# Target as fp32 on SyncE's queue, pred as bf16 on GpSimd's queue, both on the same DMA engines

## The chip, the core and the metric

The kernel runs on one core of a Trainium2 chip. The metric is the device time of one execution in microseconds (us). Engines are named as the profile names them: PE (TensorE, matmuls), PEld (its weight loads), DVE (VectorE), ACT (ScalarE), POOL (GpSimd), SP (SyncE). A DMA is issued from a queue, here SP's or POOL's, and moved by the core's 16 DMA engines.

## What is computed

Masked-patch reconstruction loss for 32 samples of 147 rows with 768 elements each, with the target normalised per row:

```python
mean = target.mean(axis=-1, keepdims=True)
var = target.var(axis=-1, keepdims=True)
target = (target - mean) / np.sqrt(var + 1e-6)
loss = np.mean((pred - target) ** 2, axis=-1)   # (32, 147)
return loss.mean(axis=-1)                       # (32,)
```

pred and target are fp32, 14.45 MB each. A sum of squares over everything is wanted, one number per sample.

## The kernel before

**Layout.** The 147 rows of a sample are spread over four partitions, 37 rows each for the first three and 36 for the fourth, so that 32 samples fill 128 partitions. "Column" c (0 to 35) is the c-th row of every partition: 128 x 768 elements. Column 36, called `REST` (`KM` = 36 is the same number), exists on 96 partitions only. All of target and pred has room in SBUF, so no load waits for a buffer.

**Work on one column.** DVE takes `bn_stats` over two halves of 384 and `bn_aggr` (mean, variance), for a *group* of columns; ACT takes the Sqrt of the group's variances; DVE makes 1/sqrt (`r`) and -mean/sqrt (`nmr`); that is `stats(g)`. POOL normalises a column to bf16, s = t * r + nmr (`normalise`). For a *unit* of two columns (the last two and `REST` are units of one) PE forms z = p - s in PSUM by matmuls against a negative and a positive identity (`subtract`: three matmuls on s, three on p for a pair), and ACT squares z and sums it along the row (`square`). Small matmuls against a mask add the partitions of a sample (`sums`), DVE adds up, and SP stores 32 numbers. PSUM holds two z at a time; the `work` pool holds ten normalised units.

**Loads.** Each piece of one to four columns is one DMA; each of its partition rows is contiguous in DRAM (12 KB for four fp32 columns). Only two pieces, target's `REST` and columns 0 to 3, go over SP's queue, as fp32. All others are issued by POOL, which casts fp32 to bf16 on the way: four bytes are read for two written. The list `stream` alternates target and pred pieces, target some eight columns ahead, and ends with smaller pieces. POOL's loads share eight completion semaphores in turn, so a ninth load waits for the first to land; `lanes` in the planner models that.

**Order.** Every instruction is pinned to the order of the program. A planner in Python computes a due time for each step from modelled landings (`land`) and modelled durations, collects the steps with `at(when, fn)`, and emits them sorted by due time. So what runs on each engine, and what stands behind what in its queue, follows from the modelled landings, not from the actual ones. POOL's queue holds loads and normalisations together; ACT's holds the Sqrts and the squares together.

Of the kernel before, what the change touches and what calls it, by code (L numbers as in the profile page):

```python
# [7 lines left out]
F32 = mybir.dt.float32  # L8
BF16 = mybir.dt.bfloat16
# [5 lines left out]
def kernel(  # L15
# [7 lines left out]
    nc = tc.nc  # L23
    pin = tc.keep_in_program_order
    B, N, D = pred.shape
    eps = 1e-6
    P = 128
    J = P // B
    KJ = (N + J - 1) // J
    KM = N - (J - 1) * KJ  # L30
# [4 lines left out]
    REST = KM  # L35
# [4 lines left out]
    def rows_of(c):  # L40
        return RP if c == REST else P

    def dram(x, c0, c1):
        return bass.AP(tensor=x.tensor, offset=x.offset + c0 * D,
                       ap=[[N * D, B], [KJ * D, J - 1 if c0 == REST else J], [1, (c1 - c0) * D]])

    data = ctx.enter_context(tc.tile_pool(name="data", bufs=1))
# [4 lines left out]
    psum1 = ctx.enter_context(tc.tile_pool(name="psum1", bufs=1, space=bass.MemoryType.PSUM))  # L52


    stream = [("t", REST, REST + 1, "hw"), ("t", 0, 4, "hw"), ("p", REST, REST + 1, "sw")]
    stream += [("t", 4, 8, "sw"), ("t", 8, 12, "sw"), ("p", 0, 4, "sw")]
    for c in range(12, KM - 4, 4):
        stream += [("t", c, c + 4, "sw"), ("p", c - 8, c - 4, "sw")]
    stream += [("t", KM - 4, KM - 2, "sw"), ("p", KM - 12, KM - 8, "sw"), ("t", KM - 2, KM, "sw"),
               ("p", KM - 8, KM - 6, "sw"), ("p", KM - 6, KM - 4, "sw"), ("p", KM - 4, KM - 2, "sw"),  # L60
               ("p", KM - 2, KM - 1, "sw"), ("p", KM - 1, KM, "sw")]

    units = [(REST,)] + [(c, c + 1) for c in range(0, KM - 2, 2)] + [(KM - 2,), (KM - 1,)]

    groups = [(REST,)] + [tuple(range(c, c + 4)) for c in range(0, KM - 8, 4)]
    groups += [(c, c + 1) for c in range(KM - 8, KM, 2)]


    land, issue = {}, []
    t = 2.7  # L70
    for kind, c0, c1, q in stream:
        t += (c1 - c0) * D * 4 * rows_of(c0) / 430e3
        issue.append(t + 1.0)
        for c in range(c0, c1):
            land[kind, c] = t + 1.0

    todo = []

    def at(when, fn):
        todo.append((when, len(todo), fn))  # L80

    tbuf, pbuf, sbuf, rs = {}, {}, {}, {}

    def load(kind, c0, c1, q):
        x = targ_f if kind == "t" else pred_f
        n = rows_of(c0)
        til = data.tile([P, (c1 - c0) * D], F32 if q == "hw" else BF16, name=f"{kind}{c0}")
        eng = nc.sync if q == "hw" else nc.gpsimd
        pin(eng.dma_start(out=til[:n], in_=dram(x, c0, c1)))  # L89
        for c in range(c0, c1):  # L90
            (tbuf if kind == "t" else pbuf)[c] = (til, (c - c0) * D)

    lanes = [0.0] * 8
    k = 0
    for i, piece in enumerate(stream):
        if piece[3] == "hw":
            at(-1.0, lambda piece=piece: load(*piece))
        else:
            at(lanes[k % 8] + (0.01 * k), lambda piece=piece: load(*piece))
            lanes[k % 8] = issue[i] + 0.2  # L100
            k += 1

    ident = singles.tile([P, P], BF16)
    nident = singles.tile([P, P], BF16)
# [100 lines left out]
    for u in units:  # L205
# [7 lines left out]
        i = main_units.index(u) if u in main_units else -1  # L213
# [47 lines left out]
```

## Time and profile before

| | us |
|---|---|
| median of 3 runs (81.06 to 81.78) | 81.3 |
| the profiled execution | 80.73 |
| its span, first to last instruction | 79.0 |
| busy: POOL / DVE / PE / ACT | 50.1 / 45.7 / 38.7 / 32.5 |
| share of POOL's queue in the time of 16 DMA engines | 84.2% |
| share of SP's queue | 6.2% |

How to read it: busy times are sums over the span, and no engine is above 63% of it. The profile names lines of the kernel (L140 `bn_stats`, L142 Sqrt, L144 `nmr`, L158 `normalise`, L178 `subtract`, L184 `square`, L89 the loads), the tiles by the program's names (`t`, `p`, `s`, `z`), and in brackets the idle time before an instruction with what ended it. GB/s counts the bytes that a DMA writes. In the changed kernel all lines are 12 higher, the loads excepted, which go from L89 to L106.

### The profile page before, as it was taken

Reading aid. Unit: us, or ns where it says so; the run is one execution under the profiler, and the core shown is the slowest. Engines: PE = TensorE matmul, PEld = TensorE weight load, DVE = VectorE, ACT = ScalarE, POOL = GpSimd, SP = SyncE. Lnnn points to the kernel's source line nnn. Section 1 sums busy time; section 2 is a strip of 40 time slices with the busy share of each in tenths; the row PEclk is TensorE's granted clock in tenths of the full one; section 3 lists DMA queues with packets and bytes.
Section 4 is the critical chain, followed back from the end, with each engine's and each line's share of the span. In section 5 each row is a group of like instructions: output and inputs, shape, how many; then the busy total and the mean of one; then the engine's idle time right before and its main releaser. Section 6 shows DMA issues by size and latency. Waiting matters only on the chain.

```text
span 79.0 us, 602 instructions
## 1 busy us (share of the span) xinstructions
PE 38.7 (49%) x126; PEld 13.4 (17%) x126; DVE 45.7 (58%) x137; ACT 32.5 (41%) x53; POOL 50.1 (63%) x73
## 2 busy tenths in 40 slices
PE   0000330008990069985317980991399496496500
PEld 0000210001320023231102320320131031223300
DVE  0061039979799799797797089529779267000000
ACT  5000000050100590872931760583134873999700
POOL 4998802059789899897797795399779360800000
PEclk9999999999999655599965569759956999999996
DMA  0799999999999999999999999999999999990000
GB/s 0 182 412 317 311 218 218 211 218 218 211 215 218 211 216 218 211 211 218 218 211 215 218 215 209 221 215 211 205 227 202 210 210 220 199 165 4 0 0 0
DMA packets 3444, 15.43 MB, mean 195 GB/s; under 512 B 432, under 2 KB 784, under 8 KB 3312
## 3 DMA queue, kind: packets, MB, share of 16 engines
q0 software_dynamic: 3136, 13.52, 84.2%
q1 hardware_dynamic: 304, 1.87, 6.2%
q14 instruction: 3, 0.02, 0.1%
q8 instruction: 1, 0.02, 0.1%
HBM read 28.90 MB, written 0.00 MB: 366 GB/s over the span
## 4 chain that ended last, share of the span: by engine, by line
DMA 42%; DVE 31%; ACT 7%; POOL 5%; PE 4%; issue 4%; SPq 1%; ACTq 0%
DMA p<-in_pred_dram 30%; DVE st L140 23%; DMA t<-in_target_dram 12%; DVE mv L141 5%; ACT z L184 5%; POOL s L158 5%; PE z L178 4%; ACT r L142 2%; DVE r L143 1%; DVE nmr L144 1%; SPq L89 1%; POOL t L89 1%; PE acc L190 0%; DVE ob L224 0%; ACTq L256 0%
## 5 line engine op out<-in xcount | busy, mean ns | idle before, releaser
L140 DVE BATCH_NORM_STATS2 st<-t 128x6 f32<-128x384 bf16 (+2 forms) x74 | 36.3, 533 | 14.4 <-DMA t<-in_target_dram 14.4
L158 POOL TENSOR_SCALAR s<-t,r,nmr 128x768 bf16<-128x768 bf16 (+2 forms) x37 | 35.9, 976 | 13.3 <-DVE nmr L144 13.0
L178 PE MATMUL z<-s,nident 128*128 128x512 bf16 (+3 forms) x57 | 21.4, 492 | 26.6 <-POOL s L158 23.7
L184 ACT ACTIVATE z<-z 128x1536 f32<-128x1536 f32 (+2 forms) x20 | 26.7, 1336 | 2.0 <-PE z L178 2.0
L178 PE MATMUL z<-p,ident 128*128 128x512 bf16 (+3 forms) x57 | 20.6, 478 | 8.9 <-DMA p<-in_pred_dram 8.9
L142 ACT ACTIVATE r<-mv,eps_t 128x4 f32<-128x4 f32 (+2 forms) x12 | 3.6, 296 | 39.4 <-DVE mv L141 39.4
L178 PEld LDWEIGHTS <-nident 128*128 128x128 bf16 (+1 forms) x57 | 5.8, 117 | 39.5 <-ACT z L184 16.3
L89 POOL DMA_DIRECT2D p<-in_pred_dram x13 | 7.7, 594 | 5.2 <-DMA t<-in_target_dram 3.2
L178 PEld LDWEIGHTS <-ident 128*128 128x128 bf16 (+1 forms) x57 | 7.0, 123 | 20.5 <-issue 17.8
L141 DVE BATCH_NORM_AGGREGATE mv<-st 128x2 f32<-128x12 f32 (+1 forms) x37 | 7.7, 208 | 1.3
L89 POOL DMA_DIRECT2D t<-in_target_dram x9 | 5.3, 589 | 0.0
L143 DVE RECIPROCAL r<-r 128x4 f32<-128x4 f32 (+2 forms) x12 | 2.1, 172 | 4.6 <-ACT r L142 4.6
L224 DVE TENSOR_REDUCE ob<-acc 32x1 f32<-32x15 f32 x1 | 0.2, 161 | 7.9 <-PE acc L190 7.9
L184 ACT ACTIVATION_READ_ACCUMULATOR z<-z 128x1 f32 (+1 forms) x20 | 3.7, 186 | 0.0
L144 DVE SCALAR_TENSOR_TENSOR nmr<-mv,r 128x4 f32<-128x4 f32 (+2 forms) x12 | 1.9, 161 | 0.4
L142 ACT ACT_TABLE_LOAD x1 | 1.3, 1283 | 0.8 <-PEq L242 0.8
L190 PE MATMUL acc<-rl,mask 128*32 128x1 f32 (+1 forms) x10 | 0.8, 179 | 0.8 <-ACT z L184 0.8
L190 PEld LDWEIGHTS acc<-rl,mask 128*32 128x32 f32 x10 | 0.5, 110 | 1.5 <-ACT z L184 0.9
L110 DVE MEMSET eps_t<- 128x1 f32 x1 | 0.1, 59 | 0.9 <-PEq L242 0.9
L112 POOL MEMSET ident<- 128x128 bf16 x1 | 0.4, 362 | 0.0
L113 POOL TENSOR_SCALAR_AFFINE_SELECT ident<-ident 128x128 bf16<-128x128 bf16 x1 | 0.3, 292 | 0.1
L113 POOL TENSOR_SCALAR_AFFINE_SELECT nident<-nident 128x128 bf16<-128x128 bf16 x1 | 0.3, 292 | 0.1
(13 smaller groups left out, 2.0 us busy)
## 6 DMA issues: line engine op xcount, KB each, us to landing
t<-in_target_dram POOLq DMA_DIRECT2D x7, 768.0 KB, 26.0
p<-in_pred_dram POOLq DMA_DIRECT2D x7, 768.0 KB, 26.6
t<-in_target_dram SPq DMA_DIRECT2D x1, 1536.0 KB, 9.7
p<-in_pred_dram POOLq DMA_DIRECT2D x3, 384.0 KB, 21.8
t<-in_target_dram POOLq DMA_DIRECT2D x2, 384.0 KB, 25.9
p<-in_pred_dram POOLq DMA_DIRECT2D x2, 192.0 KB, 16.4
t<-in_target_dram SPq DMA_DIRECT2D x1, 288.0 KB, 3.7
p<-in_pred_dram POOLq DMA_DIRECT2D x1, 144.0 KB, 3.7
```

The lines of the kernel that those rows point to most:

```text
L89: pin(eng.dma_start(out=til[:n], in_=dram(x, c0, c1)))
L112: pin(nc.gpsimd.memset(til, 0.0))
L113: pin(nc.gpsimd.affine_select(out=til, in_=til, compare_op=ALU.not_equal, fill=v, base=0, pattern=[[-1, P]], channel_multiplier=1))
L140: pin(nc.vector.bn_stats(out=st[:n, j, :], in_=til[:n, o + j * half:o + (j + 1) * half]))
L141: pin(nc.vector.bn_aggr(out=mv[:n, i], in_=st[:n]))
L142: pin(nc.scalar.activation(out=r[:n], in_=mv[:n, :, 1], func=ACTF.Sqrt, bias=eps_t[:n], scale=1.0))
L143: pin(nc.vector.reciprocal(out=r[:n], in_=r[:n]))
L144: pin(nc.vector.scalar_tensor_tensor(out=nmr[:n], in0=mv[:n, :, 0], scalar=-1.0, in1=r[:n], op0=ALU.mult, op1=ALU.mult))
L158: pin(nc.gpsimd.tensor_scalar(out=s[:n, so:so + D], in0=til[:n, o:o + D], scalar1=r, scalar2=nmr, op0=ALU.mult, op1=ALU.add))
L178: pin(nc.tensor.matmul(z[:n, a:b], w[:n, :n], src[:n, so + a:so + b], start=first, stop=not first))
L184: pin(nc.scalar.activation(out=z[:n, :W], in_=z[:n, :W], func=ACTF.Square, accum_out=to))
L190: pin(nc.tensor.matmul(acc[:, 0:b - a], mask, rl[:, a:b], start=a == 0, stop=b == len(main_units)))
```

## The change

- All of target is loaded as fp32 over SP's queue, in eleven DMAs issued at once at the start: columns 0 to 3, `REST`, then fours, and two pairs at the end.
- All of pred stays bf16 over POOL's queue, in nine DMAs with rows of eight columns for the first 24 columns, then smaller. The first is issued behind the first normalisation of column 0 (`P_START`).
- The planner models two queues that share 432 GB/s evenly from then on, instead of one stream. Groups and units begin with columns 0 to 7, and `REST` comes later; the end has groups of 4, 2 and 2 instead of four groups of 2.

```diff
-    stream = [("t", REST, REST + 1, "hw"), ("t", 0, 4, "hw"), ("p", REST, REST + 1, "sw")]
-    stream += [("t", 4, 8, "sw"), ("t", 8, 12, "sw"), ("p", 0, 4, "sw")]
-    for c in range(12, KM - 4, 4):
-        stream += [("t", c, c + 4, "sw"), ("p", c - 8, c - 4, "sw")]
-    stream += [("t", KM - 4, KM - 2, "sw"), ("p", KM - 12, KM - 8, "sw"), ("t", KM - 2, KM, "sw"),
-               ("p", KM - 8, KM - 6, "sw"), ("p", KM - 6, KM - 4, "sw"), ("p", KM - 4, KM - 2, "sw"),
-               ("p", KM - 2, KM - 1, "sw"), ("p", KM - 1, KM, "sw")]
-    units = [(REST,)] + [(c, c + 1) for c in range(0, KM - 2, 2)] + [(KM - 2,), (KM - 1,)]
-    groups = [(REST,)] + [tuple(range(c, c + 4)) for c in range(0, KM - 8, 4)]
-    groups += [(c, c + 1) for c in range(KM - 8, KM, 2)]
...
+    t_pieces = [(0, 4), (REST, REST + 1)] + [(c, c + 4) for c in range(4, KM - 4, 4)]
+    t_pieces += [(KM - 4, KM - 2), (KM - 2, KM)]
+    p_pieces = [(0, 8), (REST, REST + 1), (8, 16), (16, 24), (24, 28), (28, 32), (32, 34), (34, 35), (35, 36)]
+    units = [(0, 1), (2, 3), (4, 5), (6, 7), (REST,)] + [(c, c + 1) for c in range(8, KM - 2, 2)] + [(KM - 2,), (KM - 1,)]
+    groups = [(0, 1), (2, 3), (REST,)] + [tuple(range(c, c + 4)) for c in range(4, KM - 4, 4)]
+    groups += [(KM - 4, KM - 3), (KM - 2, KM - 1)]
+    P_START = 10.2
+    jobs = {"t": [2.2, list(t_pieces)], "p": [P_START + 1.3, list(p_pieces)]}
...
+        step = min(left[q] for q in live) * len(live)
...
+            left[q] -= step / len(live)
...
-        til = data.tile([P, (c1 - c0) * D], F32 if q == "hw" else BF16, name=f"{kind}{c0}")
-        eng = nc.sync if q == "hw" else nc.gpsimd
+        til = data.tile([P, (c1 - c0) * D], F32 if kind == "t" else BF16, name=f"{kind}{c0}")
+        eng = nc.sync if kind == "t" else nc.gpsimd
...
-    for i, piece in enumerate(stream):
-        if piece[3] == "hw":
-            at(-1.0, lambda piece=piece: load(*piece))
-        else:
-            at(lanes[k % 8] + (0.01 * k), lambda piece=piece: load(*piece))
+    for i, (c0, c1) in enumerate(t_pieces):
+        at(-1.0, lambda c0=c0, c1=c1: load("t", c0, c1))
+    for i, (c0, c1) in enumerate(p_pieces):
+        at(P_START + 1.5 * i, lambda c0=c0, c1=c1: load("p", c0, c1))
```

More of the change, by code (lines that the diff above doesn't have):

```diff
@@ L63 @@
-    units = [(REST,)] + [(c, c + 1) for c in range(0, KM - 2, 2)] + [(KM - 2,), (KM - 1,)]
-    groups = [(REST,)] + [tuple(range(c, c + 4)) for c in range(0, KM - 8, 4)]
-    groups += [(c, c + 1) for c in range(KM - 8, KM, 2)]
[L69 to L75, printed above, removed]
+    t_pieces = [(0, 4), (REST, REST + 1)] + [(c, c + 4) for c in range(4, KM - 4, 4)]
@@ new lines @@
+    t_pieces += [(KM - 4, KM - 2), (KM - 2, KM)]
[4 more added lines that the diff above has]
+    P_START = 10.2
+    land = {}
+    jobs = {"t": [2.2, list(t_pieces)], "p": [P_START + 1.3, list(p_pieces)]}
@@ new lines @@
+    now = 0.0
+    left = {}
+    while jobs:
+        live = [q for q in jobs if jobs[q][0] <= now]
+        if not live:
+            now = min(j[0] for j in jobs.values())
+            continue
+        for q in live:
+            if q not in left:
+                c0, c1 = jobs[q][1][0]
+                left[q] = (c1 - c0) * D * 4 * rows_of(c0) / 432e3
+        step = min(left[q] for q in live) * len(live)
+        later = [jobs[q][0] - now for q in jobs if q not in live]
+        step = min([step] + later)
+        now += step
+        for q in live:
+            left[q] -= step / len(live)
+            if left[q] < 1e-9:
+                del left[q]
+                c0, c1 = jobs[q][1].pop(0)
+                for c in range(c0, c1):
+                    land[q, c] = now + 0.9
+                if not jobs[q][1]:
+                    del jobs[q]
@@ L82, with load @@
     tbuf, pbuf, sbuf, rs = {}, {}, {}, {}
-    def load(kind, c0, c1, q):
+    def load(kind, c0, c1):
         x = targ_f if kind == "t" else pred_f
         n = rows_of(c0)
-        til = data.tile([P, (c1 - c0) * D], F32 if q == "hw" else BF16, name=f"{kind}{c0}")
-        eng = nc.sync if q == "hw" else nc.gpsimd
+        til = data.tile([P, (c1 - c0) * D], F32 if kind == "t" else BF16, name=f"{kind}{c0}")
+        eng = nc.sync if kind == "t" else nc.gpsimd
         pin(eng.dma_start(out=til[:n], in_=dram(x, c0, c1)))
@@ L91, in load @@
             (tbuf if kind == "t" else pbuf)[c] = (til, (c - c0) * D)
-    lanes = [0.0] * 8
-    k = 0
-    for i, piece in enumerate(stream):
-        if piece[3] == "hw":
-            at(-1.0, lambda piece=piece: load(*piece))
-        else:
-            at(lanes[k % 8] + (0.01 * k), lambda piece=piece: load(*piece))
-            lanes[k % 8] = issue[i] + 0.2
-            k += 1
+    for i, (c0, c1) in enumerate(t_pieces):
+        at(-1.0, lambda c0=c0, c1=c1: load("t", c0, c1))
+    for i, (c0, c1) in enumerate(p_pieces):
+        at(P_START + 1.5 * i, lambda c0=c0, c1=c1: load("p", c0, c1))
     ident = singles.tile([P, P], BF16)
```

## The prediction, written before the result was known

> **What bounds the kernel now.** I read the page's slices and DMA rows first, then the timeline of the last 15 us, then the first microseconds cut into single stretches, because the change alters who shares the DMA engines there.
>
> ```profile
> DMA  0799999999999999999999999999999999990000
> GB/s 0 182 412 317 311 218 218 211 218 218 211 215 218 211 216 218 211 211 218 218 211 215 218 215 209 221 215 211 205 227 202 210 210 220 199 165 4 0 0 0
> q0 software_dynamic: 3136, 13.52, 84.2%
> HBM read 28.90 MB, written 0.00 MB: 366 GB/s over the span
> ```
>
> The DMA engines are full from about 2.5 us to 71 us. GB/s counts what is written; on GpSimd's queue (q0) four bytes are read for two written, so 215 written is 430 read. Over the 68 us the 28.90 MB come to 425 GB/s read, and I use 0.425 MB/us for all that follows. The change reads the same bytes, so the transfers as a whole cannot end earlier; what can move is the order of landing, and what the engines still have to do after it.
>
> ```profile
> 63.97 1.02 DVE L140 BATCH_NORM_STATS2 st<-t 128x6 f32<-128x384 bf16 x2 [1.70 <-DMA t<-in_target_dram]
> 66.45 0.29 ACT L142 ACTIVATE r<-mv,eps_t 128x2 f32<-128x2 f32 x1 [1.66 <-DVE mv L141]
> 66.66 1.43 ACT L184 ACTIVATE z<-z 128x1536 f32<-128x1536 f32 x1
> ...
> 68.11 1.43 ACT L184 ACTIVATE z<-z 128x1536 f32<-128x1536 f32 x1
> ...
> 69.83 1.44 ACT L184 ACTIVATE z<-z 128x1536 f32<-128x1536 f32 x1 [0.17 <-PE z L178]
> ...
> 71.28 1.44 ACT L184 ACTIVATE z<-z 128x1536 f32<-128x1536 f32 x1
> ...
> 72.72 0.80 ACT L184 ACTIVATE z<-z 128x768 f32<-128x768 f32 x1
> ...
> 73.80 0.80 ACT L184 ACTIVATE z<-z 128x768 f32<-128x768 f32 x1 [0.16 <-PE z L178]
> ```
>
> This sets the end. Target columns 34 and 35 land at 63.97; their statistics take until 66.45; only then does the last Sqrt (L142) run on ScalarE. Every later square (L184) stands behind it: ScalarE sat 1.66 us before it, although PE's data for the first square was ready at 64.86 (matmuls at 64.05, 0.81 us). From the Sqrt to the end ScalarE never stops: four pair squares and two singles, 66.45 to 74.8, one pair every 1.54 us ((71.28-66.66)/3). So the end is "start of the last Sqrt, plus the squares queued behind it". Pred is all down by about 72 us and is not what is waited for. That is the sum I redo below.
>
> ```profile
> 5.00:6.00 1.00, 0.00 (x0) 0.00 (x0) 0.73 (x3) 0.20 (x1) 1.00 (x3) 1.00 0.98 412
> 6.00:7.00 1.00, 0.00 (x0) 0.03 (x1) 0.31 (x2) 0.10 (x1) 0.84 (x5) 1.00 1.03 319
> 7.00:8.00 1.00, 0.00 (x0) 0.12 (x1) 0.00 (x0) 0.00 (x0) 0.74 (x5) 1.00 1.02 295
> 8.00:9.00 1.00, 0.00 (x0) 0.00 (x0) 0.00 (x0) 0.00 (x0) 1.00 (x2) 1.00 1.03 319
> 9.00:10.00 1.00, 0.82 (x3) 0.56 (x3) 0.00 (x0) 0.00 (x0) 0.67 (x2) 1.00 1.03 319
> 11.00:12.00 1.00, 0.00 (x0) 0.00 (x0) 0.74 (x2) 0.00 (x0) 0.00 (x0) 1.00 1.02 209
> ```
>
> The last two figures are DMA share and GB/s. At 5 us SyncE's fp32 piece runs alone (412). From 6 to 10 both queues run, 313 on average: if SyncE's queue gets h and GpSimd's s, h + s/2 = 313 and h + s = 420 give h = 206, s = 214: an even split. In that stretch both sent rows of 12 KB (four columns), so it doesn't tell a split by packets from one by bytes.
>
> **What the Trainium skill says.** "DMA: Bandwidth & Descriptors", section "Queues, rings and completion order": each DMA engine goes round the queues that have work and takes a whole packet from one before it switches. The trace agrees as far as it goes (even split at equal rows); its packet counts fit one packet per row: q0's 3136 are the 2784 rows of its 22 loads plus 16 completions each. Same page, "Issuing engines are not separate DMA queues": a second queue adds no bandwidth; here 420 both, 430 one. "TensorE: Matmul & The Clock Gate", section on the array's architecture: ScalarE and VectorE are strict FIFO; the Sqrt at 66.45 shows it.
>
> **The change, part by part.**
>
> (1) *Compute.* Counts are unchanged: 74 statistics, 37 normalisations, 20 squares. On fp32 the statistics took 532 ns and the normalisation 974, on bf16 532 and 977 (rows by form): zero. POOL sheds 13 DMA issues of 0.59 us, 7.7 us in all, but it idles before normalisations (13.0 us on nmr), so this buys nothing.
>
> (2) *Target alone at the start.* Piece 0-3 lands at 7.2 instead of 11.26 (1.57 MB / 0.425 = 3.7, plus 3.5 for start and receipt: the landing at 63.97 in before, after 25.75 MB, gives 63.97-60.6 = 3.4). VectorE begins 4 us earlier. But it needs only 5.3 us per group of four and is fed slower than that later, so the lead is spent waiting.
>
> (3) *Pred behind the first column.* Stats of columns 0,1 end near 10, normalise 0 at 11.2, issue 11.2. First data: 1.4 us after its issue for the first GpSimd load of before (3.7 to landing, less 1.4 transfer and 0.9 receipt), 4 us for the second (issued 2.04; HW alone until 6). I take 2.3: 13.5 us; ends 12.6 and 15.2. By then target has 10.9 x 0.425 = 4.63 MB.
>
> (4) *The shared stretch.* Pred now comes in rows of 8 columns (24 KB read), target in rows of 12 KB. If turns go by packet, pred takes 2/3. Pred 0-7 (3.15 MB) with 1.57 MB of target: 4.72/0.425 = 11.1 us, to 24.6, target at 6.2. Pred's rest column (0.295 MB, 3 KB rows, one fifth) with 1.18 of target: 3.5, to 28.1, 7.4. Pred 8-15: 39.2, 8.95. Pred 16-23: 50.3, 10.5. Pred 24-27 in 12 KB rows, even: 7.4, to 57.7, 12.1. Target 28-31 is complete at 12.87 MB: 0.78/0.2125 = 3.7, 61.3, landed 62.2 (before: 52.94). Target 34-35, carried on the same way through the smaller rows, lands at 70.1 (before: 63.97). The rate itself is open too, since fp32 rows alone ran at 412 and cast rows alone at 430: 0.412 would add 2.1 us to the whole (28.9/0.412 against 68), 0.43 take off 0.8.
>
> (5) *Order on ScalarE and VectorE.* The order that the new planner writes out puts Sqrt 28-31, one pair square, Sqrt 32-33, two pair squares, Sqrt 34-35, and behind that six pairs and two singles. Before had four pairs behind it: +2 x 1.54 = +3.1 us. The last Sqrt starts at the latest of three: target 28-31 landed + 10.7 (4 x 1.13 statistics, Sqrt and nmr 0.7, two pairs of columns at 2.26 with another 0.7 between, and 0.3 of gaps); target 34-35 landed + 2.5 (63.97 to 66.45); pred 16-23 landed + 5.6 (three matmuls 0.9, three squares 4.35, Sqrt 0.3). By packets: 62.2+10.7 = 72.9; 70.1+2.5 = 72.6; 51.2+5.6 = 56.8. So 72.9 against 66.45: +6.5.
>
> (6) *Waits that are new.* The ninth pred load waits for the first one's landing (about 25 us); behind it on POOL stand the normalisations of columns 5, 6, 7 and all later ones, for whom PE waits, but PE has no pred before that landing either: nothing lost. SyncE's ninth to eleventh target loads wait for the first three landings, long past.
>
> Sum: +6.5 + 3.1 = +9.6, so 80.73 + 9.6 = 90.3 for the profiled execution. Its start and tail (1.7 us outside the span, output DMA) stay. The runs' median, 81.3, is 0.6 above it; I put the forecast between, at 90.6. Start of pred from 12.6 to 15.2 gives +10.4 to +8.8.
>
> **The rivals.**
>
> *Even by bytes* (or 24 KB rows are cut into smaller packets, so that the change does what its own schedule assumes). Then target 28-31 lands at 53.2, 34-35 at 60.6, pred 16-23 at 60.2. Last Sqrt: 63.9, 63.1, 65.8. The third rules, and a smaller share for pred costs hardly more (at the latest it lands at (14.45+9.73)/0.425+3.5 = 60.4): Sqrt 32-33 waits in ScalarE's queue behind square 16,17, which waits for pred. 65.8-66.45+3.1 = +2.4: 83.1 to 83.7. If PE comes to that burst at the lower clock (512 columns 0.43 us each instead of 0.22, as at 29-32 us of before), up to +4. For it: the even split of 6 to 10 us. Against: it was between equal rows.
>
> *Not slower: the two queues together move more.* The place is 13.5 to 70 us, the mechanism that fp32 rows need no cast and fill gaps of the cast rows. Under an even split the third term must fall to 63.3 (66.45-3.1) for no change: pred 16-23 landed at 57.7, so 19.46 MB of both in 43.3 us, 0.449 MB/us; over 1% faster needs 0.458. At 0.465: -1.5 us; 79.5 between the two bases. For it: one half-microsecond near 449 in the fp32 phase. Against: 420 over 6 to 10 us with both, 412 alone.
>
> **How the numbers follow.** By packet 0.58 (90.6; own range 88.8 to 92.2), even 0.24 (83.5), more bandwidth 0.08 (79.5), the remaining 0.10 for a split still worse for target (two thirds also at equal rows, over 92) or between. The range 82.8 to 92.2 holds the first two. Within 1% is about what a measurement of this kernel can tell from no change. Slower 0.91; same 0.04, faster 0.05, mostly from the third case and the low edge of the second.
>
> **What would show it.** In the profile after: pred 0-7 landing near 25.5 and target 12-15 near 26.6 (even: 29.2 and 23.6); long VectorE idle before L152 released by target, over 15 us in all; last Sqrt (L154) near 73 with six pairs behind it; GB/s near 283 in 14-24 us (1/3 + 2/3 x 1/2 of 425; even: 319). I am wrong if the shared stretch shows 319, if target ends before 62 us, or if the end is not ScalarE's queue.

## The result, and the profile after

The changed kernel takes 91.75 us (median of four runs, 91.63 to 91.80) against 81.3; the ratio is 1.1275, interval 1.122 to 1.133. The profiled execution has a span of 90.0 us against 79.0. Forecast were 90.6 us, with a range of 82.8 to 92.2.

The page first: DMA and GB/s by slices of 2.25 us, the queues, and the shares of the chain that ended last.

```profile
DMA  0999999998989998998998999999999800000000
GB/s 16 311 389 364 431 431 431 284 311 235 322 268 384 317 322 268 262 333 262 273 322 257 295 287 330 300 328 281 268 304 295 154 1 7 0 4 0 0 0 0
...
q1 hardware_dynamic: 1600, 14.45, 39.9%
q0 software_dynamic: 1264, 7.23, 38.7%
...
HBM read 28.90 MB, written 0.00 MB: 321 GB/s over the span
...
DMA t<-in_target_dram 54%; DVE st L152 13%; ACT z L196 6%; SPq L106 5%; PE z L190 4%; DVE mv L153 3%; ACT r L154 1%; DVE r L155 1%; DVE nmr L156 1%; PE acc L202 0%; DVE ob L236 0%; ACTq L268 0%; ACTq L154 0%; ACTq L196 0%
```

The same 28.90 MB are read, and the transfers end in the 32nd slice, near 71 us, as before. Most of the extra 11 us of span stand after that: eight nearly empty slices of 2.25 us, where before had four of 1.98. The chain no longer hangs on pred (30% before) but on target (54%). q0's 1264 packets are pred's 1120 rows plus 16 for each of its nine loads, so a row of 24 KB went as one packet.

The shared stretch, from the windows of the kernel after (PEclk, DMA share and GB/s written are the last three figures):

```profile
14.00:15.00 1.00, 0.74 (x2) 0.15 (x1) 0.97 (x3) 0.00 (x0) 0.98 (x3) 1.00 0.99 418
15.00:16.00 1.00, 0.00 (x0) 0.00 (x0) 0.60 (x4) 0.29 (x1) 1.00 (x2) 1.00 1.02 418
16.00:18.00 2.00, 0.00 (x0) 0.00 (x0) 1.97 (x5) 0.00 (x0) 1.96 (x3) 1.00 1.13 289
18.00:20.00 2.00, 0.00 (x0) 0.00 (x0) 1.93 (x7) 0.00 (x0) 2.00 (x5) 1.00 0.91 283
20.00:24.00 4.00, 0.00 (x0) 0.00 (x0) 3.50 (x12) 0.30 (x1) 1.40 (x2) 1.00 1.03 289
```

Until 16 us target runs alone. From then on some 287 GB/s are written. With 425 read in all and h for target, h + (425-h)/2 = 287 gives h = 149: target gets 35%, pred 65%. The mix is there from the first 2 us on (289, where pred alone would write about 215), so a turn is much shorter than a whole load of eight columns, which would take 7.4 us by itself (3.15/0.425). The landings show what that does to VectorE (its timeline, those lines that target released):

```profile
26.89 1.02 DVE L152 BATCH_NORM_STATS2 st<-t 128x6 f32<-128x384 f32 x2 [0.32 <-DMA t<-in_target_dram]
...
43.24 1.02 DVE L152 BATCH_NORM_STATS2 st<-t 128x6 f32<-128x384 f32 x2 [2.97 <-DMA t<-in_target_dram]
...
54.01 1.02 DVE L152 BATCH_NORM_STATS2 st<-t 128x6 f32<-128x384 f32 x2 [5.39 <-DMA t<-in_target_dram]
...
61.41 1.02 DVE L152 BATCH_NORM_STATS2 st<-t 128x6 f32<-128x384 f32 x2 [1.97 <-DMA t<-in_target_dram]
...
70.80 1.02 DVE L152 BATCH_NORM_STATS2 st<-t 128x6 f32<-128x384 f32 x2 [0.61 <-DMA t<-in_target_dram]
```

These are columns 12, 20, 24, 28 and 34; the last landed at 63.97 before. And the end, on ScalarE's timeline:

```profile
73.28 0.30 ACT L154 ACTIVATE r<-mv,eps_t 128x2 f32<-128x2 f32 x1 [0.60 <-DVE mv L153]
73.48 1.43 ACT L196 ACTIVATE z<-z 128x1536 f32<-128x1536 f32 x1
...
74.94 1.43 ACT L196 ACTIVATE z<-z 128x1536 f32<-128x1536 f32 x1
...
76.66 1.44 ACT L196 ACTIVATE z<-z 128x1536 f32<-128x1536 f32 x1 [0.17 <-PE z L190]
...
78.42 1.44 ACT L196 ACTIVATE z<-z 128x1536 f32<-128x1536 f32 x1 [0.22 <-ACT z L196]
...
79.86 1.44 ACT L196 ACTIVATE z<-z 128x1536 f32<-128x1536 f32 x1
...
81.58 1.44 ACT L196 ACTIVATE z<-z 128x1536 f32<-128x1536 f32 x1 [0.17 <-PE z L190]
...
83.02 0.80 ACT L196 ACTIVATE z<-z 128x768 f32<-128x768 f32 x1
...
84.10 0.80 ACT L196 ACTIVATE z<-z 128x768 f32<-128x768 f32 x1 [0.16 <-PE z L190]
```

The last Sqrt starts at 73.28 instead of 66.45 (+6.83), and from there to the end of the last square it takes 11.62 us instead of 8.15 (+3.47): six pairs stand behind it, not four.

### The profile page after: what moved, and what is told of

It reads as the page before. It is cut to its first block, busy times and chain, and to the rows that moved or that the text cites. A ratio compares the mean times of both kernels' runs of the same rounds, so it can differ in the third digit from the quotient of the medians.

```text
span 90.0 us, 608 instructions
## 1 busy us (share of the span) xinstructions
PE 38.7 (43%) x126; PEld 13.3 (15%) x126; DVE 48.7 (54%) x137; ACT 32.5 (36%) x53; POOL 42.9 (48%) x60
## 3 DMA queue, kind: packets, MB, share of 16 engines
q0 software_dynamic: 1264, 7.23, 38.7%
HBM read 28.90 MB, written 0.00 MB: 321 GB/s over the span
## 4 chain that ended last, share of the span: by engine, by line
DMA 54%; DVE 17%; ACT 8%; SPq 5%; PE 4%; issue 3%; another core or an unknown queue 3%; ACTq 0%
DMA t<-in_target_dram 54%; DVE st L152 13%; ACT z L196 6%; SPq L106 5%; PE z L190 4%; DVE mv L153 3%; ACT r L154 1%; DVE r L155 1%; DVE nmr L156 1%; PE acc L202 0%; DVE ob L236 0%; ACTq L268 0%; ACTq L154 0%; ACTq L196 0%
## 5 line engine op out<-in xcount | busy, mean ns | idle before, releaser
L170 POOL TENSOR_SCALAR s<-t,r,nmr 128x768 bf16<-128x768 f32 (+1 forms) x37 | 35.9, 982 | 27.0 <-DVE nmr L156 25.4
L152 DVE BATCH_NORM_STATS2 st<-t 128x6 f32<-128x384 f32 (+1 forms) x74 | 36.3, 532 | 18.3 <-DMA t<-in_target_dram 18.1
L106 POOL DMA_DIRECT2D p<-in_pred_dram x9 | 5.2, 587 | 5.2 <-DMA p<-in_pred_dram 5.2
L156 DVE SCALAR_TENSOR_TENSOR nmr<-mv,r 128x4 f32<-128x4 f32 (+2 forms) x12 | 4.8, 403 | 0.4
## 6 DMA issues: line engine op xcount, KB each, us to landing
p<-in_pred_dram POOLq DMA_DIRECT2D x1, 144.0 KB, 18.1
```

Source lines behind the costliest of these rows:

```text
L152: pin(nc.vector.bn_stats(out=st[:n, j, :], in_=til[:n, o + j * half:o + (j + 1) * half]))
L156: pin(nc.vector.scalar_tensor_tensor(out=nmr[:n], in0=mv[:n, :, 0], scalar=-1.0, in1=r[:n], op0=ALU.mult, op1=ALU.mult))
L170: pin(nc.gpsimd.tensor_scalar(out=s[:n, so:so + D], in0=til[:n, o:o + D], scalar1=r, scalar2=nmr, op0=ALU.mult, op1=ALU.add))
```

## The experiments

The explanation to be tested: the DMA engines take turns by packet, one packet is one row, and pred's rows are twice as long as target's; so target starves, and the order on ScalarE adds to it. Rival one: the split is by bytes or by time, and it is the doubled fp32 writes that cost. Rival two: all of it is the order on ScalarE. Times are medians; the kernel before measured 81.4 us beside the first four, 81.1 beside the others.

**Rows of 12 KB for pred** (`e1_p12`).

```diff
-    for i, (c0, c1) in enumerate(p_pieces):
-        at(P_START + 1.5 * i, lambda c0=c0, c1=c1: load("p", c0, c1))
+    p_loads = [(0, 4), (4, 8), (REST, REST + 1), (8, 12), (12, 16), (16, 20), (20, 24), (24, 28), (28, 32), (32, 34), (34, 35), (35, 36)]
+    p_times = [10.2, 10.21, 11.7, 13.2, 13.21, 14.7, 14.71, 16.2, 30.0, 37.0, 38.0, 45.0]
+    for when, (c0, c1) in zip(p_times, p_loads):
+        at(when, lambda c0=c0, c1=c1: load("p", c0, c1))
```

> Pred's three 8-column loads are cut into two 4-column loads each, so that its rows are 12 KB like target's; the order on VectorE, ScalarE and PE stays as in the changed kernel, the last four pred loads are issued later so that POOL does not block on them. Turns by packet: an even split, about 319 GB/s written in the shared stretch, target 28-31 lands near 49 (61.4 in the changed kernel), target 34-35 near 60 (70.8); pred 16-19 now lands by itself near 55, so the last Sqrt comes near 63 and the time near 83. Turns by bytes or time, or the doubled fp32 writes as the cause: the split and the writes stay as they are, 289 GB/s and within 2 us of 91.75, save what finer landings of pred give.

Measured: 83.22 us, 1.024 of before (1.020 to 1.027). Windows, DVE and ACT lines of this kernel:

```profile
18.00:26.00 8.00, 2.15 (x6) 0.76 (x6) 7.40 (x22) 0.30 (x1) 6.09 (x8) 1.00 1.02 320
...
61.46 1.02 DVE L154 BATCH_NORM_STATS2 st<-t 128x6 f32<-128x384 f32 x2 [1.94 <-DMA t<-in_target_dram]
...
62.26 1.44 ACT L198 ACTIVATE z<-z 128x1536 f32<-128x1536 f32 x1 [1.78 <-PE z L192]
...
63.94 0.30 ACT L156 ACTIVATE r<-mv,eps_t 128x2 f32<-128x2 f32 x1
```

320 GB/s is the even split (h = 215). Target 34-35 lands 9.3 us earlier, the last Sqrt starts at 63.94, 9.3 us earlier too, and 8.5 of the 10.3 us are back. As many fp32 bytes are written as in the changed kernel. So the length of pred's rows was the main cause; this run may also profit from pred's finer landings, which the next run leaves out.

**Rows of 24 KB for target** (`e2_t24`). This gives equal rows the other way round; pred's loads are untouched.

```diff
-    for i, (c0, c1) in enumerate(t_pieces):
+    for c0, c1 in [(0, 4), (REST, REST + 1), (4, 8), (8, 16), (16, 24), (24, 32), (32, 34), (34, 36)]:
         at(-1.0, lambda c0=c0, c1=c1: load("t", c0, c1))
```

> Pred untouched; six of target's 4-column loads merged into three of 8 columns, so that both queues send rows of 24 KB. The order of instructions on VectorE, ScalarE, PE and POOL is that of the changed kernel line for line. Turns by packet: even split again, about 319 GB/s; pred 0-7 lands near 31 instead of 27.3, target 34-35 near 62.5; the end is set by pred 16-23 landing near 59-60, time 84 to 86. Turns by bytes or time: no change in the split; coarser landings of target can only cost, 92 or more.

Measured: 84.65 us, 1.042 (1.038 to 1.045). Windows and PE's timeline:

```profile
18.00:26.00 8.00, 0.00 (x0) 0.00 (x0) 5.60 (x18) 0.30 (x1) 3.53 (x6) 1.00 1.00 307
16.00:30.00 14.00, 0.00 (x0) 0.00 (x0) 11.06 (x33) 0.59 (x2) 5.49 (x8) 1.00 1.03 327
...
31.43 1.44 PE L190 MATMUL z<-p,ident 128*128 128x512 bf16 x3 [16.58 <-DMA p<-in_pred_dram]
...
60.03 0.81 PE L190 MATMUL z<-p,ident 128*128 128x512 bf16 x3 [1.61 <-DMA p<-in_pred_dram]
```

Pred 0-7 lands at 31.4 as forecast (27.34 in the changed kernel), pred 16-23 at 60.0, and 7.1 us are back with not one instruction of the compute engines or POOL in another place. Longer target rows, coarser landings, less time: that excludes a split by bytes, and one by time too, since neither would change with the cut of target's loads. (307 is the mean of 18 to 26 us, 327 that of 16 to 30; the next run comes back to the difference.)

**Rows of 6 KB for target** (`e3_t6`), the same edit with `[(0, 4), (REST, REST + 1)] + [(c, c + 2) for c in range(4, KM, 2)]`.

> Pred untouched; target after column 3 in 2-column loads, rows of 6 KB against pred's 24 KB. Turns by packet: pred gets four fifths while its 24 KB rows last, about 255 GB/s written (0.2 + 0.8/2 of 425); pred 0-7 lands near 24, pred 16-23 near 44, target 28-31 near 67, time 96 to 98. Turns by bytes or time: 91.75 within 1 us.

Measured: 97.67 us, 1.202 (1.199 to 1.205). Windows and VectorE:

```profile
18.00:26.00 8.00, 0.62 (x2) 0.25 (x2) 7.04 (x21) 0.60 (x2) 3.60 (x7) 1.00 1.02 266
30.00:40.00 10.00, 4.43 (x11) 1.64 (x12) 5.97 (x18) 4.75 (x7) 7.03 (x8) 1.00 1.04 262
...
37.92 1.02 DVE L152 BATCH_NORM_STATS2 st<-t 128x6 f32<-128x384 f32 x2 [3.46 <-DMA t<-in_target_dram]
...
46.72 1.02 DVE L152 BATCH_NORM_STATS2 st<-t 128x6 f32<-128x384 f32 x2 [6.41 <-DMA t<-in_target_dram]
```

266 gives target a quarter (h = 107); a fifth was forecast at 255. Over the ratios of row lengths, pred to target, of 1 (e1, e2), 2 (after) and 4 (e3), these windows give target 51 and 44, 35 and 25%; turns by packet say 50, 33, 20. The windows are no sharper than that: with 16 to 30 instead of 18 to 26, e2 has 54% (327), and with 30 to 40 this run has 23% (262). The two landings above are 8.8 us apart for 0.79 MB of target, 21% of 425.

Sharpest are the single packets, which the traces record with queue, size and time. In the kernel after, pred's 128 rows of columns 8 to 15 went from 30.56 to 42.01 and target's 128 rows of columns 20 to 23 from 30.98 to 42.01; in this run the same pred rows went from 27.05 to 36.70 and target's 128 rows of columns 16 and 17 from 27.18 to 36.61. Within these stretches the starts come in batches of 16, as many as there are DMA engines, pred and target by turns. That is one row from each queue a turn, 12 KB or 6 KB against 24. A row's length and the size of its load change together in all these runs; the batches are what tells a turn by rows from a turn by whole loads.

The last Sqrt of this run is at 79.38, 6.1 us after that of the changed kernel, and the time is 5.9 us longer: the same order behind it, moved as a whole.

**The planner told of the split** (`e4_replan`). The loads stay; only the order changes.

```diff
-    jobs = {"t": [2.2, list(t_pieces)], "p": [P_START + 1.3, list(p_pieces)]}
+    jobs = {"t": [2.2, list(t_pieces)], "p": [P_START + 4.5, list(p_pieces)]}
...
-        step = min(left[q] for q in live) * len(live)
+        share = {q: jobs[q][1][0][1] - jobs[q][1][0][0] for q in live}
+        total = sum(share.values())
+        step = min(left[q] * total / share[q] for q in live)
...
-            left[q] -= step / len(live)
+            left[q] -= step * share[q] / total
```

> Loads as in the changed kernel; only the planner's model of the split follows the row sizes (2/3 to pred at 8 columns against 4) and lets pred start 4.5 us after its issue, so that the order on the engines changes: three pairs and two singles stand behind the last Sqrt instead of six and two, and the two Sqrts before the end follow each other. Target lands as late as in the changed kernel (34-35 near 70). If the share alone is the cost: about 91. If the order behind the Sqrt is a cost of its own, as the prediction has it (1.54 us a pair): three pairs less, 4.6 us, about 87.

Measured: 88.71 us, 1.092 (1.084 to 1.099): 3.0 us less than the changed kernel, not 4.6. VectorE and ScalarE:

```profile
71.63 1.02 DVE L154 BATCH_NORM_STATS2 st<-t 128x6 f32<-128x384 f32 x2 [1.37 <-DMA t<-in_target_dram]
...
74.12 0.29 ACT L156 ACTIVATE r<-mv,eps_t 128x2 f32<-128x2 f32 x1 [4.32 <-DVE mv L155]
...
74.51 1.44 ACT L198 ACTIVATE z<-z 128x1536 f32<-128x1536 f32 x1
...
75.95 1.44 ACT L198 ACTIVATE z<-z 128x1536 f32<-128x1536 f32 x1
...
78.40 1.44 ACT L198 ACTIVATE z<-z 128x1536 f32<-128x1536 f32 x1 [0.89 <-PE z L192]
```

Three pairs stand behind the Sqrt, as planned; but target 34-35 landed at 71.63 in this execution (70.80 in the changed kernel, with the same loads), so that the Sqrt is 0.84 later, and ScalarE waits 0.89 for PE within the rest: 4.6 - 0.84 - 0.89 is 2.9. So order is a cost of its own, about a third of what equal rows took back, and rival two falls as the sole cause: with the order mended the kernel is still 7.3 us behind before. No run mends rows and order together.

**Before, with one square moved** (`f1_before_swap`). It tests my reading of the end of the kernel before.

```diff
+        last_stats = dve
...
-        at(act, lambda u=u: square(u))
+        at(min(act, last_stats - 0.01) if u == (KM - 10, KM - 9) else act, lambda u=u: square(u))
```

> The kernel before, with one change: on ScalarE the square of columns 26 and 27 goes ahead of the last Sqrt (columns 34, 35) instead of behind it. Its data was ready at 64.86 and ScalarE idle from 64.8 to 66.45, so the square fits into that gap and one pair fewer stands behind the Sqrt. If the end is the Sqrt plus the squares behind it, up to 1.5 us less, bounded by pred's last landings near 71 to 72 with some 2 us behind them: 80.0 to 80.8. If the end is pred's landing or PE, no change: 81.3 to 81.4.

Measured over 22 runs: 80.93 against 81.09, ratio 0.998 (0.996 to 1.000). It missed: at most 0.4% where 0.6 to 1.6% was expected. The profiled execution took 81.97, above that median, so its time is not compared with before; its waits are these (VectorE, PE and ScalarE):

```profile
65.60 1.02 DVE L140 BATCH_NORM_STATS2 st<-t 128x6 f32<-128x384 bf16 x2 [1.70 <-DMA t<-in_target_dram]
...
67.50 0.81 PE L178 MATMUL z<-p,ident 128*128 128x512 bf16 x3 [0.20 <-DMA p<-in_pred_dram]
...
68.09 0.30 ACT L142 ACTIVATE r<-mv,eps_t 128x2 f32<-128x2 f32 x1
...
69.33 0.59 PE L178 MATMUL z<-p,ident 128*128 128x512 bf16 x2 [0.33 <-DMA p<-in_pred_dram]
...
72.12 1.44 ACT L184 ACTIVATE z<-z 128x1536 f32<-128x1536 f32 x1 [0.34 <-PE z L178]
```

Here the Sqrt no longer waits, and PE waits for pred twice near the end, with a square waiting for PE later on. That would fit an end at which pred's last landings are next in line. But target 34-35 landed 1.6 us later here than in the profile of before (63.97), so this execution doesn't show what took up the gain in the others. What the run shows is that a pair taken from behind the last Sqrt of the kernel before was worth 0.16 us (0.3 at most) and not up to 1.5; the reason is open.

**First pred load at the start** (`e5_early`), `at(P_START + 1.5 * i if i else -1.0, ...)` in the pred loop.

> The changed kernel, with only the first pred load (columns 0 to 7) issued at the very start instead of behind the first normalised column. It takes two turns in three from then on: target 0-3 lands after 8 us instead of 7.8 if the load needs 4 us from issue to its first data also on idle DMA engines, and near 13 us if it needs 1.4 there. Target is late all the way (28-31 near 65 to 67, 61.4 in the changed kernel): 95 to 98. If the place of the first pred load did not matter: 91.75.

Measured: 95.90 us, 1.184 (1.181 to 1.187). Windows and VectorE:

```profile
4.00:5.00 1.00, 0.00 (x0) 0.00 (x0) 0.00 (x0) 0.00 (x0) 0.30 (x2) 1.00 0.99 418
5.00:6.00 1.00, 0.00 (x0) 0.00 (x0) 0.00 (x0) 0.00 (x0) 0.00 (x0) 1.00 1.13 406
6.00:7.00 1.00, 0.00 (x0) 0.00 (x0) 0.00 (x0) 0.00 (x0) 0.00 (x0) 1.00 0.85 221
...
10.24 1.02 DVE L152 BATCH_NORM_STATS2 st<-t 128x6 f32<-128x384 f32 x2 [9.30 <-DMA t<-in_target_dram]
```

Issued at 1.32, its data show only from 6 us: over 4 us, though no transfer ran yet when it was issued (target's own began near 2). Target 0-3 lands at 10.24, between my two guesses. Placing pred behind the first column is worth 4.1 us at these row lengths; it is not what made the change slow.

**Pred's small rest load at the start** (`e6_restfirst`), the same edit for the rest load only.

> The changed kernel, with pred's small rest load (96 rows of 3 KB) issued at the very start, and columns 0 to 7 behind the first normalised column as before. It asks where the 4 us from issue to first data come from (the prediction took 2.3). If only the first load on POOL's queue pays them: written bytes drop from 418 to 290 GB/s about 1.5 us after the issue of columns 0 to 7, near 13.5, pred 0-7 lands near 25. If every 128-row load beside a busy queue needs 4 us: the drop stays near 16 and pred 0-7 lands at 27 to 28. The small load itself costs target 0.3 us at the start, and is missing later, where its 3 KB rows gave target four turns in five by bytes: in both cases target 28-31 comes up to 3 us later, 92 to 95.

Measured: 93.60 us, 1.154 (1.148 to 1.160).

```profile
15.00:16.00 1.00, 0.00 (x0) 0.00 (x0) 0.60 (x3) 0.29 (x1) 1.00 (x2) 1.00 1.16 406
16.00:18.00 2.00, 0.00 (x0) 0.00 (x0) 1.97 (x6) 0.00 (x0) 1.95 (x4) 1.00 0.97 252
```

The load of columns 0 to 7, issued at 11.99, again begins near 16. So it is not only the first load on POOL's queue that pays 4 us. The rest load itself is in the lists of DMA issues of before and of this run (the last figure is the time from issue to landing):

```profile
p<-in_pred_dram POOLq DMA_DIRECT2D x1, 144.0 KB, 3.7
p<-in_pred_dram POOLq DMA_DIRECT2D x1, 144.0 KB, 7.3
```

It was issued at 1.36 in both, but here it took 3.6 us longer to land, and by the packet records its first row began at 5.76 instead of 3.39: 4.4 us after the issue, not 2.0. So neither the 128 rows nor the size of a load decides. What differs is SP's queue: in before it began with target's `REST`, here with columns 0 to 3. That this is the reason is not shown. The time went up 1.9 us, as forecast; target 28-31 came at 64.44 (61.41 in the changed kernel). That target misses the turns that it had beside pred's 3 KB rows fits this, but no run isolates it.

## Why the prediction was right

- **Bytes and rate.** Transfers end near 71 us in both; nearly the whole loss stands behind them. Right.
- **Step 1, compute.** Statistics 532 ns, normalisation 982 on fp32 (974 and 977 forecast from): nothing gained or lost.
- **Step 2, target alone.** Columns 0-3 land at 7.80, 7.2 forecast.
- **Step 3, the start of pred, was mis-sized.** 2.3 us from issue to first data were taken, with 4 as the upper end; it was 4.0 (issue 11.95, data from 16.0), 2.5 us later than 13.5 as the issue was late too, and beyond the upper end of 15.2. e5 and e6 show the same 4 us. The short value, 1.4, was taken from pred's rest load in before; its packets give 2.0 there, and 4.4 for the same load in e6, so that it was no property of the load.
- **Step 4, the split, carried it.** 283 GB/s forecast, 287 measured; target 28-31 at 62.2, measured 61.41; target 34-35 at 70.1, measured 70.80. Pred 0-7 at 25.5, measured 27.34, is step 3 again. e1, e2 and e3 show that the row length decides. The Trainium skill's sentence in "DMA: Bandwidth & Descriptors", section "Queues, rings and completion order", that an engine takes a whole packet before it switches, agrees with this case: 128 rows of pred beside 128 of target, at 2 to 1 as at 4 to 1. Of the signs that the prediction named, one told little: VectorE's idle time released by target was 18.1 us (over 15 forecast), but it is 14.4 in before.
- **Step 5, the order.** Last Sqrt 72.9 forecast, 73.28 measured, but through the term that the prediction had second: the Sqrt waited for target 34-35 (70.80 + 2.48; forecast were 70.1 + 2.5). The path from target 28-31, which was to rule, had VectorE free 0.61 us before that. Two more pairs were to cost 3.1 and cost 3.47, with three gaps of about 0.2 us among the six pairs where before had one. e4 gained 3.0 from three pairs fewer, not 4.6; a later landing and a wait for PE took the rest.
- **Step 6.** POOL waited 5.23 us for the first pred landing. VectorE and PE had no use for its work before; no trace of it at the end.
- **The sum.** +9.6 forecast for the profiled execution; the last addition for `ob` starts 10.29 later (85.31 against 75.02), of which 6.83 is the Sqrt and 3.47 the queue behind it. The span grew by 11.0; the output's DMA, 3.4 us to landing instead of 2.9, has most of the rest. The closeness is in part luck: by the prediction's own sum a start of pred at 15.2 gives +8.8, and it started at 16.0. Part of what offset it were the 0.4 us of gaps and a smaller head start of target: the page's first four slices come to 2.4 MB by 9 us, where (9 - 2.6) x 0.425 = 2.7 were taken. The rest is not taken apart.
- **The rivals.** The even split was worked out as 83.1 to 83.7 for these loads; with it, e1 came out at 83.22 and e2, with coarser target loads, 1 us above at 84.65. More bandwidth from two queues: the transfers end when they did. The 420 that the prediction held against it for 6 to 10 us had been put into its sum of the split, not read from a line; with 430 the same sum gives target 46%, which is still near even.
- **What was too simple.** "ScalarE never stops, so the Sqrt sets the end" describes the trace of before, but doesn't say what would follow if that queue got shorter: f1 gained at most 0.4%. It didn't touch the forecast: in the changed kernel the transfers end near 71 us, and the squares behind the Sqrt run until 84.9.

None of the runs beats the kernel before by more than its uncertainty; f1 comes nearest. With the DMA engines full until 71 us in before and 4 us behind that, another order of loads can win some 4 us at most.

## What to carry to other kernels

When two queues share the DMA engines, compare the bytes of one row on each: here the queue with rows twice as long took about two thirds (65%), whichever was needed first. Give the stream that feeds the longest chain of engines rows at least as long as the other's: equal rows took back 7.1 and 8.5 of the 10.3 us here and were still 2 to 4% slower than before; longer rows for that stream were not run. And where a planner writes out the order of an in-order engine, a wrong share in its model is paid a second time, as work that is ready but stands behind a wait: here 3 us on top.

## What the runs showed that I had not expected

- Loads of columns 0 to 7 from POOL took about 4 us from issue to first data (11.95 to 16.0 in the kernel after, 1.32 to 6 in e5, 11.99 to 16 in e6), whether transfers ran at the issue or not. The small rest load, which had seemed quick, was as slow in e6, where target's columns 0 to 3 went first on SP's queue (4.4 us to its first row, 2.0 in before).
- One `nmr` instruction of the kernel after took 2.87 us instead of 0.16 (at 32.11, while POOL ran normalisations back to back). VectorE waited for target after it (2.97 us at 43.24), so it cost nothing; its cause is open.
- The turns held to the row over whole loads, 128 rows of each queue in the same 11 us, while the rate over a window of 8 us moved target's share by some ten points (e2: 44% or 54%).
